# Scan layer of a hybrid decoder trunk: masked products in column pairs with the decay matrix moving, copied out and turned back

## The chip, the cores and the metric

The kernel runs on one core of one Trainium2 chip. The metric is the device time of one launch in microseconds, lower is better. The core's engines are TensorE (PE in the profile, with its weight loads on a row of their own, PEld), VectorE (DVE), ScalarE (ACT), GpSimd (POOL) and SyncE (SP). Each works through its own instructions in the order in which the program lists them; where two engines depend on each other, the later one waits on a semaphore. So an instruction that waits also holds back everything listed behind it on the same engine.

## What is computed

The trunk has two layers of 256 tokens and 1024 features: feed-forward, mixer, feed-forward, each followed by a layer norm. The mixer of the first layer is sparse attention, that of the second a Mamba-2 scan with 32 heads of 64 features in 4 groups of 8 heads, computed in two chunks of 128 tokens. The part that matters here:

```python
    cb = jnp.einsum('bclgn,bcsgn->bcgls', cm, bm)
    y_diag = jnp.einsum('bcgrls,bcsgrp->bclgrp', cb[:, :, :, None] * decay, xdt)
    ...
    y_off = jnp.einsum('bclgn,bcgrpn->bclgrp', cm, prev) * jnp.exp(a_cs_l)[..., None]
    return (y_diag + y_off).reshape(bsz, seq, n_h, p_dim)
...
    y = y + xs.astype(jnp.float32) * d_skip.astype(jnp.float32)[:, None]
    yz = y.reshape(bsz, seq, SSM_INNER) * jax.nn.silu(z.astype(jnp.float32))
    yz = yz.reshape(bsz, seq, SSM_GROUPS, SSM_INNER // SSM_GROUPS)
    yz = yz * lax.rsqrt(jnp.mean(jnp.square(yz), -1, keepdims=True) + RMS_EPS)
```

`y_diag` is, for every head and chunk, a 128x128 matrix (decay times `cb`, masked to the lower triangle) times a 128x64 matrix of inputs. All values are float32.

## The kernel before

Weights come from DRAM as float32 tiles of 128x1024 ("units"). Each unit is split into a high part `wh` (a cast on ACT, line 326, or line 324 where a scale goes in) and a low part `wl` (a subtraction on DVE, line 354 or 351; for a few units ACT negates the raw tile, line 332, and a DMA adds to it). A projection then takes three products instead of one (lines 539, 540 and 541). Ten units may be split ahead of their use. This splitting is most of the work of ACT and DVE, and it is spread over the program by calls of `W.pump`.

The scan layer is the function `ssd`. Its last stage is a loop over the four groups `g`, in an order that is written out by hand. Two threads run through it. One is long projection work for PE, in pieces called fillers, `f[0]` to `f[7]`: for groups 0 and 1 four projections of input tiles for the next group (`xs_tile`, 24 matmuls of 256 columns, ended by a convolution on ACT and DVE in `conv`) and four halves of the gate projection (`z_half`, 12 matmuls of 512 columns); for group 2 a mixture of input tiles and output products (`out_piece`, 12 matmuls of 512 columns); for group 3 output products alone. The other thread is the group's own chain, for the two token tiles t = 0 and 1, placed between the fillers:

- `x_tok` turns the group's inputs to tokens by features and makes `y[t]` (inputs times dt) and `xd[t]` (inputs times the skip factor).
- `decay_load`, `decay_seg`, `decay_exp` and `decay_cb` make the masked decay matrix `M[t, g]`, 128 x (8 heads x 128), by a DMA from POOL's queue, DVE, ACT and DVE.
- `diag` multiplies: for each head the 128x128 slice of `M` is the stationary operand, 64 columns of `y[t]` move, and the result lands with tokens on the partitions.
- `carry` adds what the first chunk hands to the second: one matmul, then two DVE operations on `xe` and `xd[1]`.
- `gate` (DVE) adds `diag`'s result in PSUM to `xd[t]` and multiplies by the gate; `square` (ACT) sums squares; `root` (POOL, two operations) makes the inverse root; `norm` (ACT) scales.
- `y_tr` turns the result back on PE with four transposes and splits it (`yH` on ACT, `yL` on DVE, lines 535 and 536) for the output products.

In PSUM the helper `ptr` hands out two banks in turn, `pmm` two others, and `acc00` to `acc11` are four single ones; at the end the output products accumulate in all four `acc` banks. From group 2 on, `out_piece(0)` therefore needs `acc11`, which `x_tok(0, g)` uses for g < 3.

Of the kernel before, what the change touches and what calls it, by code (L numbers as in the profile page):

```python
# [11 lines left out]
F32 = mybir.dt.float32  # L12
# [400 lines left out]
def trunk_kernel(ctx: ExitStack, tc: tile.TileContext, widths, forms, x, ln_g, ln_b, wts, kvg, convp,  # L413
                 dt_bias, a_log, d_skip, norm_g, out):
    nc = tc.nc
# [5 lines left out]
    psum = ctx.enter_context(tc.tile_pool(name="psum", bufs=1, space=bass.MemoryType.PSUM))  # L421
# [4 lines left out]
    def nm(s):  # L426
        cnt[0] += 1
        return f"{s}_{cnt[0]}"

    def f4(s):  # L430
        return wk.tile([128, 1024], F32, name=nm(s), tag="f4", bufs=12)

    def f2(s):
        return wk.tile([128, 512], F32, name=nm(s), tag="f2", bufs=9)
# [4 lines left out]
    def r2(s):  # L439
        return wk.tile([128, 512], F32R, name=nm(s), tag="r2", bufs=10)  # L440

    def tiny(s, n=32):
        return wk.tile([128, n], F32, name=nm(s), tag=f"tiny{n}", bufs=14 if n == 32 else 4)
# [4 lines left out]
    def pmm():  # L448
        return psum.tile([128, 512], F32, name=nm("pmm"), tag="pmm", bufs=2)
# [11 lines left out]
    def ptr():  # L461
        return psum.tile([128, 512], F32, name=nm("ptr"), tag="ptr", bufs=2)
# [22 lines left out]
    ident = consts.tile([128, 128], F32, name="ident")  # L485
# [35 lines left out]
    def rsqrt_pool(src, eps, scale=1.0):  # L521

        n = src.shape[1]
        e = tiny("rse")
        nc.gpsimd.tensor_scalar(e[:, :n], src, float(scale), float(eps), op0=ALU.mult, op1=ALU.add)
        return power_pool(e[:, :n])
# [7 lines left out]
    def split_psum(H, L, ps):  # L534
        nc.scalar.copy(H, ps)
        nc.vector.tensor_sub(L, ps, H.bitcast(F32))  # L536
# [841 lines left out]
    def ssd(xT, u, ln_i):  # L1378
# [85 lines left out]
        def z_half(g, t, i, uu):  # L1464

            if not i:
                zps[t] = ptr() if t and g == 1 else pmm()
            ps = zps[t]
            for k in range(4 * i, 4 * i + 4):
                H, L = W.get(uu + k // 2)  # L1470
                c = slice((k % 2) * 512, (k % 2 + 1) * 512)
                sl = slice(t * 128, (t + 1) * 128)
                mm3(ps, xT.H[:, k, sl], xT.L[:, k, sl], H[:, c], L[:, c], k == 0, k == DK - 1)
                if t and k % 2:
                    W.free(uu + k // 2)
            if i:
                if not t:
                    zs[g] = f4("zs")
                nc.scalar.activation(zs[g][:, t * 512:(t + 1) * 512], ps, AF.Silu)
# [3 lines left out]
        def decay_load(t, g):  # L1483
            M[t, g] = f4("M")
            nc.gpsimd.dma_start(M[t, g], scr[t:t + 1, g * 8:(g + 1) * 8, :].rearrange("o h l -> o (h l)")
                                .to_broadcast([128, 1024]))
# [49 lines left out]
        def hv(ap):  # L1536
            return ap.rearrange("p (h d) -> p h d", h=8)

        def hb(ap, g):
            return ap[:, g * 8:(g + 1) * 8][:, :, None].to_broadcast([128, 8, 64])  # L1540

        def decay_seg(t, g):

            mv = M[t, g].rearrange("p (h l) -> p h l", h=8)
            nc.vector._custom_dve(TENSOR_ADD_SAT, out=mv, in0=mv, s0=0.0, s1=-3e38,
                                  in1=nacs[t][:, g * 8:(g + 1) * 8][:, :, None].to_broadcast([128, 8, 128]))
# [7 lines left out]
                                 .to_broadcast([128, 8, 128]))  # L1554

        yT = {}
        y, xd, xe, ss = {}, {}, {}, {}

        def x_tok(t, g):

            if t:
                pt = ptr()
            elif g < 3:
                pt = psum.tile([128, 512], F32, name=nm("pxt"), tag="acc11", bufs=1)
            else:
                pt = pmm()
            for i in range(4):
                nc.tensor.transpose(pt[:, i * 128:(i + 1) * 128], xsT[g][i][:, t * 128:(t + 1) * 128], ident)
            y[t], xd[t] = f2("xdt"), f2("xtok")
            nc.vector.tensor_mul(hv(y[t]), hv(pt), hb(dt[:, t * 32:(t + 1) * 32], g))  # L1570
            nc.vector.tensor_mul(hv(xd[t]), hv(pt), hb(dsk, g))
# [3 lines left out]
            nc.vector.tensor_mul(hv(xe[g]), hv(y[0]), hb(dend, g))  # L1575

        def diag(t, g):
            m = M.pop((t, g))
            py = psum.tile([128, 512], F32, name=nm("py"), tag="acc11", bufs=1) if t and g < 2 else ptr()
            for h in range(8):  # L1580
                nc.tensor.matmul(py[:, h * 64:(h + 1) * 64], m[:, h * 128:(h + 1) * 128],
                                 y[t][:, h * 64:(h + 1) * 64], start=True, stop=True)
            return py

        def carry(g):

            po = ptr()
            nc.tensor.matmul(po, cross[:, g * 128:(g + 1) * 128], xe[g], start=True, stop=True)
            nc.vector.tensor_mul(hv(xe[g]), hv(po), hb(eacs, g))
            nc.vector.tensor_add(xd[1], xd[1], xe[g])  # L1590

        def gate(t, g, py):
            nc.vector.tensor_add(y[t], py, xd[t])
            nc.vector.tensor_mul(y[t], y[t], zs[g][:, t * 512:(t + 1) * 512])

        def square(t):
            ss[t] = tiny("ss")
            nc.scalar.activation(xd[t], y[t], AF.Square, accum_out=ss[t][:, 0:1])

        def root(t):  # L1600
            ss[t] = rsqrt_pool(ss[t][:, 0:1], RMS_EPS, 1.0 / 512)

        def norm(t):
            nc.scalar.activation(y[t], y[t], AF.Copy, scale=ss[t])

        def y_tr(t, g):
            pt = ptr()
            for i in range(4):
                nc.tensor.transpose(pt[:, i * 128:(i + 1) * 128], y[t][:, i * 128:(i + 1) * 128], ident)
            yT[g, t] = (r2("yH"), r2("yL"))  # L1610
            split_psum(*yT[g, t], pt)

        def xs_tile(g, i, uu):
            if not i:
                xsT[g] = []
            ps = xbank() if g < 3 else pmm()
            proj_b(ps[:, :256], xT, uu, False)
            W.free(uu)
            o = wk.tile([128, 256], F32, name=nm("xsT"), tag="xsT", bufs=5)
            conv(ps, g * 4 + i, o)  # L1620
            xsT[g].append(o)
            W.pump(1)

        def out_piece(k, uu):
            if not acc:
                acc.update(accs())
            for t in range(2):
                H, L = yT[k // 4, t]
                s = slice(k % 4 * 128, (k % 4 + 1) * 128)
                out_k(acc, t, H[:, s], L[:, s], uu, k == 0, False)  # L1630
            W.free(uu)
            W.pump(1)
# [40 lines left out]
        decay_exp(1, 0)  # L1673
        W.lows()
        u += 4
        py = {}
        for g in range(SG):
            if g < 2:
                f = [lambda i=i: xs_tile(g + 1, i, u + i) for i in range(4)]
                f += [lambda t=t, i=i: (z_half(g + 2, t, i, u + 4), W.pump(1)) for t in range(2) for i in range(2)]  # L1680
            elif g == 2:
                x3 = [lambda i=i: xs_tile(3, i, u + 2 * i) for i in range(4)]
                o0 = [lambda i=i: out_piece(i, u + 2 * i + 1) for i in range(4)]
                f = [x3[0], x3[1], o0[0], x3[2], o0[1], x3[3], o0[2], o0[3]]
            else:
                f = [lambda i=i: out_piece(4 + i, u + i) for i in range(6)]
            f[0]()
            if g:
                x_tok(0, g)
                x_tok(1, g)  # L1690
            else:
                decay_cb(0, 0)
                decay_cb(1, 0)
            x_end(g)
            f[1]()
            f[2]()
            py[0] = diag(0, g)
            gate(0, g, py[0])
            carry(g)
            if g < 3:  # L1700
                decay_load(0, g + 1)
            f[3]()
            square(0)
            root(0)
            py[1] = diag(1, g)
            gate(1, g, py[1])
            if g < 3:
                decay_load(1, g + 1)
            f[4]()
            norm(0)  # L1710
            square(1)
            root(1)
            if g < 3:
                decay_seg(0, g + 1)
            f[5]()
            y_tr(0, g)
            norm(1)
            if g < 3:
                decay_seg(1, g + 1)
                f[6]()  # L1720
                flush()
                y_tr(1, g)
                decay_exp(0, g + 1)
                decay_exp(1, g + 1)
                f[7]()
                decay_cb(0, g + 1)
                decay_cb(1, g + 1)
                W.lows()
                u += 8
# [56 lines left out]
```

## Time and profile before

| | us |
|---|---|
| median of 3 runs (lowest to highest) | 1010.6 (1009.81 to 1010.91) |
| span of the profiled execution | 1009.0 |
| PE busy | 999.1 (99%) |
| PE weight loads busy | 845.8 (84%) |
| DVE busy | 905.3 (90%) |
| ACT busy | 662.0 (66%) |
| POOL busy | 109.8 (11%) |
| group loop of the scan: first `diag` to last `y_tr` | 708.7 to 812.9 in the span |

The span is measured from the first to the last instruction of one profiled execution; the runs are timed without the profiler, and their median lies 1.6 us above that span. No time of its own is listed for the profiled execution. The profile's chain of work says which engine each stretch of the span waited on; its timeline lists instructions with start, duration and, in brackets, how long the engine had been idle and who released it. A matmul's duration in such a row includes its way through the array, so what a stream of matmuls costs is read from the starts of successive rows. One float32 matmul of the program appears as two rows' worth of matmuls in the trace (8 heads are x16).

### The profile page before, as it was taken

To read this page: it belongs to the slowest core of one execution; us is meant where nothing else is said; L and a number is where in the kernel's file an instruction comes from. 1 tells how busy PE (TensorE), PEld (TensorE's weight loads), DVE (VectorE), ACT (ScalarE), POOL (GpSimd) and SP (SyncE) were. 2 spreads that over 40 slices of the span, in tenths; PEclk is the share of its full clock that TensorE was granted. 3 is DMA by queue.
4 is the path that set the end of the run, shared out by engine and by line. 5 is a ranking of instruction groups with operands and counts; after the bars stand their busy time and mean duration, and the time that the engine had idled before them with its cause. 6 is when DMAs were issued, how large, how long until landed. Compare 5 with 4: busy or idle time off the path is not lost.

```text
span 1009.0 us, 14555 instructions
## 1 busy us (share of the span) xinstructions
PE 999.1 (99%) x5273; PEld 845.8 (84%) x5273; DVE 905.3 (90%) x1224; ACT 662.0 (66%) x968; POOL 109.8 (11%) x149
## 2 busy tenths in 40 slices
PE   9999999999999999999999999999999999999997
PEld 6888888898788888888888888999888888888886
DVE  7899999888898999999899998788989978899996
ACT  6676776476755767764576776486876645676670
POOL 0010110100000101100010110150221100010100
PEclk9999999999999999999999999999999999999999
DMA  9799889551754998995499889457765754699981
GB/s 347 224 289 284 240 254 334 195 172 57 245 173 126 274 280 241 260 390 183 123 281 288 243 253 357 168 179 241 222 215 181 235 191 136 170 265 285 289 254 42
DMA packets 66055, 231.69 MB, mean 230 GB/s; under 512 B 8112, under 2 KB 9136, under 8 KB 65984
## 3 DMA queue, kind: packets, MB, share of 16 engines
q1 hardware_dynamic: 54288, 189.84, 51.7%
q0 software_dynamic: 11120, 40.41, 21.7%
q8 instruction: 41, 0.67, 0.3%
q10 hardware_dynamic: 576, 0.52, 0.2%
q14 instruction: 30, 0.25, 0.1%
HBM read 193.48 MB, written 1.08 MB: 193 GB/s over the span
## 4 chain that ended last, share of the span: by engine, by line
PE 94%; DVE 3%; DMA 1%; issue 1%; POOL 0%; ACT 0%; DVEq 0%; POOLq 0%; SPq 0%
PE pmm L539 12%; PE pmm L540 12%; PE pmm L541 12%; PE acc L539 10%; PE acc L541 10%; PE acc L540 10%; PE ptr L539 2%; PE ptr L541 2%; PE ptr L540 2%; PE pxs L539 2%; PE pxs L541 2%; PE pxs L540 2%; PE pmm L705 1%; PE ptr L705 1%; PE ptr L795 1%; PE pmm L685 1%
## 5 line engine op out<-in xcount | busy, mean ns | idle before, releaser
L354 DVE TENSOR_TENSOR wl<-raw,wh 128x1024 fp32r<-128x1024 f32 (+3 forms) x424 | 495.5, 1211 | 14.6 <-ACT wh L326 14.1
L326 ACT CAST wh<-raw 128x1024 fp32r<-128x1024 f32 (+2 forms) x431 | 428.8, 1043 | 91.8 <-DVE raw L293 51.1
L539 PE MATMUL acc<-wh,hH 128*128 128x512 f32 (+1 forms) x352 | 138.1, 392 | 0.0
L541 PE MATMUL acc<-wh,hL 128*128 128x512 f32 (+1 forms) x352 | 136.5, 388 | 0.0
L540 PE MATMUL acc<-wl,hH 128*128 128x512 f32 (+1 forms) x352 | 136.3, 387 | 0.0
L539 PE MATMUL pmm<-wh,xT 128*128 128x512 f32 (+2 forms) x304 | 119.2, 392 | 0.0
L541 PE MATMUL pmm<-wh,xT 128*128 128x512 f32 (+2 forms) x304 | 116.9, 384 | 0.0
L540 PE MATMUL pmm<-wl,xT 128*128 128x512 f32 (+2 forms) x304 | 116.7, 384 | 0.1
L266 POOL DMA_DIRECT2D raw<-raw x64 | 55.8, 877 | 490.3 <-DVE raw L293 260.4
L541 PE MATMUL pmm<-wh,xf 128*128 128x512 f32 x256 | 99.6, 389 | 0.0
L539 PE MATMUL pmm<-wh,xf 128*128 128x512 f32 x256 | 99.6, 389 | 0.0
L540 PE MATMUL pmm<-wl,xf 128*128 128x512 f32 x256 | 99.6, 389 | 0.0
L541 PEld LDWEIGHTS acc<-wh,hL 128*128 128x128 f32 x352 | 66.1, 188 | 13.7
L293 DVE TENSOR_TENSOR raw<-raw,raw 128x1024 f32<-128x1024 f32 x64 | 77.0, 1218 | 0.2
L540 PEld LDWEIGHTS acc<-wl,hH 128*128 128x128 f32 x352 | 66.2, 188 | 12.9
L539 PEld LDWEIGHTS acc<-wh,hH 128*128 128x128 f32 x352 | 66.1, 188 | 12.8
L541 PEld LDWEIGHTS pmm<-wh,xT 128*128 128x128 f32 x304 | 57.0, 188 | 11.9 <-DVE xT L536 0.5
L540 PEld LDWEIGHTS pmm<-wl,xT 128*128 128x128 f32 x304 | 57.2, 188 | 11.0 <-DVE wl L354 0.8
L539 PEld LDWEIGHTS pmm<-wh,xT 128*128 128x128 f32 x304 | 57.1, 188 | 10.0
L541 PEld LDWEIGHTS pmm<-wh,xf 128*128 128x128 f32 x256 | 48.0, 188 | 10.0
L539 PEld LDWEIGHTS pmm<-wh,xf 128*128 128x128 f32 x256 | 48.0, 188 | 10.0
L540 PEld LDWEIGHTS pmm<-wl,xf 128*128 128x128 f32 x256 | 48.0, 188 | 10.0
(321 smaller groups left out, 1784.6 us busy)
## 6 DMA issues: line engine op xcount, KB each, us to landing
raw<-in_wts_dram SPq DMA_DIRECT2D x338, 512.0 KB, 5.9
raw<-raw POOLq DMA_DIRECT2D x64, 512.0 KB, 5.4
M<-scr POOLq DMA_DIRECT2D x8, 512.0 KB, 6.0
lng<-in_ln_g_dram SPq DMA_DIRECT2D x6, 512.0 KB, 5.5
lnb<-in_ln_b_dram SPq DMA_DIRECT2D x6, 512.0 KB, 5.9
wl<-raw POOLq DMA_DIRECT2D x5, 512.0 KB, 5.5
raw<-in_wts_dram SPq DMA_DIRECT2D x4, 408.0 KB, 5.4
out_dram<-x SPq DMA_DIRECT2D x4, 256.0 KB, 2.0
```

The lines of the kernel that those rows point to most:

```text
L266: self.nc.gpsimd.dma_start(self.raw[r], self.raw[other], accum_op=ALU.add)
L293: self.nc.vector.tensor_add(self.raw[r], self.raw[r], self.raw[other])
L326: nc.scalar.copy(h[:, c:c + n], raw[:, c:c + n])
L354: self.nc.vector.tensor_sub(lo[:, s], raw[:, s], h[:, s].bitcast(F32))
L539: nc.tensor.matmul(ps, lh, rh, start=first, stop=False, skip_group_check=on)
L540: nc.tensor.matmul(ps, lh, rl, start=False, stop=False, skip_group_check=on)
L541: nc.tensor.matmul(ps, ll, rh, start=False, stop=last, skip_group_check=on)
L685: nc.tensor.matmul(ps, a, b[:, c], start=k == i == 0, stop=k == DK - 1 and i == 2)
L705: nc.tensor.matmul(ps, H[:, k * 128:(k + 1) * 128], xT.HL[:, k, :], start=k == 0, stop=False)
L795: nc.tensor.transpose(v[:, i, t * 128:(t + 1) * 128], hs[t][:, i * 128:(i + 1) * 128], ident)
```

## The change

`diag` swaps its operands. Now 64 columns of `y[t]` are stationary and the 128x128 slice of `M` moves; even heads write partitions 0 to 63 and odd heads 64 to 127 of the same PSUM columns. The result therefore lands with features on the partitions. ACT copies it from PSUM to a new tile `ydT` (`turned[t]`), and a new function `back` turns it with four transposes into another PSUM bank, from which `gate` reads. `diag(0)` and `diag(1)` now stand together before `carry`; both `decay_load`s follow them at once; `back(0)`, `back(1)` and both gates, squares and roots stand behind `f[3]`; both `norm`s behind `f[4]`; and for g < 3 `y_tr(0)` and `y_tr(1)` both stand behind `f[5]`. Of the PSUM banks, `x_tok(0, 2)` moves from `acc11` to `ptr`, and `diag(1, g)` takes `pmm` for g of 2 and 3.

```diff
-        y, xd, xe, ss = {}, {}, {}, {}
+        y, xd, xe, ss, turned = {}, {}, {}, {}, {}
...
             if t:
                 pt = ptr()
-            elif g < 3:
+            elif g < 2:
                 pt = psum.tile([128, 512], F32, name=nm("pxt"), tag="acc11", bufs=1)
             else:
-                pt = pmm()
+                pt = ptr() if g < 3 else pmm()
...
         def diag(t, g):
+
             m = M.pop((t, g))
-            py = psum.tile([128, 512], F32, name=nm("py"), tag="acc11", bufs=1) if t and g < 2 else ptr()
-            for h in range(8):
-                nc.tensor.matmul(py[:, h * 64:(h + 1) * 64], m[:, h * 128:(h + 1) * 128],
-                                 y[t][:, h * 64:(h + 1) * 64], start=True, stop=True)
+            if not t:
+                py = ptr()
+            else:
+                py = psum.tile([128, 512], F32, name=nm("py"), tag="acc11", bufs=1) if g < 2 else pmm()
+            for j in range(4):
+                for h in (2 * j, 2 * j + 1):
+                    p0 = (h % 2) * 64
+                    nc.tensor.matmul(py[p0:p0 + 64, j * 128:(j + 1) * 128], y[t][:, h * 64:(h + 1) * 64],
+                                     m[:, h * 128:(h + 1) * 128], start=True, stop=True)
+            turned[t] = f2("ydT")
+            nc.scalar.copy(turned[t], py)
+
+        def back(t):
+            a, py = turned.pop(t), ptr()
+            for j in range(4):
+                nc.tensor.transpose(py[:, j * 128:(j + 1) * 128], a[:, j * 128:(j + 1) * 128], ident)
             return py
...
             f[2]()
-            py[0] = diag(0, g)
-            gate(0, g, py[0])
-            carry(g)
+            diag(0, g)
+            diag(1, g)
             if g < 3:
                 decay_load(0, g + 1)
+                decay_load(1, g + 1)
+            carry(g)
             f[3]()
-            square(0)
-            root(0)
-            py[1] = diag(1, g)
-            gate(1, g, py[1])
-            if g < 3:
-                decay_load(1, g + 1)
+            py = [back(0), back(1)]
+            for t in range(2):
+                gate(t, g, py[t])
+                square(t)
+                root(t)
             f[4]()
             norm(0)
-            square(1)
-            root(1)
+            norm(1)
             if g < 3:
                 decay_seg(0, g + 1)
             f[5]()
             y_tr(0, g)
-            norm(1)
             if g < 3:
+                y_tr(1, g)
                 decay_seg(1, g + 1)
                 f[6]()
                 flush()
-                y_tr(1, g)
                 decay_exp(0, g + 1)
                 decay_exp(1, g + 1)
                 f[7]()
```

How the instructions then stand is shown for group 1 on the two engines between `f[3]` and `y_tr`. First ACT before, from the convolution's first step of `f[3]` (line 1498) to the cast of `y_tr(0, 1)`: line 1598 is `square`, line 1604 `norm`, `xdt` is `y[t]`, `zs` the gate of a filler.

```order
L1498 ACTIVATE cv_7486<-pxs_7460,convp_sb 128x256
L1493 ACTIVATE xsT_7430<-cv_7431 128x256
L324 ACTIVATE wh_7495<-raw_7310,ng_sb 128x1024
L1598 ACTIVATE xtok_7354,ss_7498<-xdt_7353 128x512
L326 CAST wh_7533<-raw_7400 128x1024
L1604 ACTIVATE xdt_7353<-xdt_7353,rs_7502 128x512
L1598 ACTIVATE xtok_7363,ss_7537<-xdt_7362 128x512
L1479 ACTIVATE zs_7556<-pmm_7517 128x512
L324 ACTIVATE wh_7561<-raw_7438,ng_sb 128x1024
L535 CAST yH_7569<-ptr_7564 128x512
```

The same stretch of ACT in the changed kernel, where line 1590 is the copy of `diag`'s result, 1611 `square` and 1617 `norm`:

```order
L1590 COPY ydT_7466<-ptr_7457 128x512
L1590 COPY ydT_7477<-py_7468 128x512
L1498 ACTIVATE cv_7513<-pxs_7487,convp_sb 128x256
L1493 ACTIVATE xsT_7444<-cv_7445 128x256
L324 ACTIVATE wh_7522<-raw_7324,ng_sb 128x1024
L1611 ACTIVATE xtok_7368,ss_7537<-xdt_7367 128x512
L1611 ACTIVATE xtok_7377,ss_7545<-xdt_7376 128x512
L326 CAST wh_7567<-raw_7414 128x1024
L1617 ACTIVATE xdt_7367<-xdt_7367,rs_7541 128x512
L1617 ACTIVATE xdt_7376<-xdt_7376,rs_7549 128x512
L1479 ACTIVATE zs_7585<-pmm_7551 128x512
L324 ACTIVATE wh_7590<-raw_7452,ng_sb 128x1024
```

The cast of `y_tr(0, 1)` follows. The two copies are new, and `norm` of tile 0, which stood behind the first square alone, now stands behind both squares. DVE before, from the last weight of `f[2]` to the second gate (lines 1593 and 1594 are `gate`, 1589 and 1590 `carry`, 1501 the three further steps of a convolution):

```order
L351 SCALAR_TENSOR_TENSOR wl_7403<-raw_7271,ng_sb,wh_7402 128x1024
L1593 TENSOR_TENSOR xdt_7353<-ptr_7443,xtok_7354 128x512
L1594 TENSOR_TENSOR xdt_7353<-xdt_7353,zs_6344 128x512
L1589 TENSOR_TENSOR xe_7366<-ptr_7454,eacs_6238 128x512
L1590 TENSOR_TENSOR xtok_7363<-xtok_7363,xe_7366 128x512
L1501 SCALAR_TENSOR_TENSOR cv_7486<-pxs_7460,convp_sb,cv_7486 128x255
L1501 SCALAR_TENSOR_TENSOR cv_7486<-pxs_7460,convp_sb,cv_7486 128x254
L1501 SCALAR_TENSOR_TENSOR cv_7486<-pxs_7460,convp_sb,cv_7486 128x253
L354 TENSOR_TENSOR wl_7441<-raw_7302,wh_7440 128x1024
L1593 TENSOR_TENSOR xdt_7362<-py_7504,xtok_7363 128x512
L1594 TENSOR_TENSOR xdt_7362<-xdt_7362,zs_6344 128x512
```

DVE in the changed kernel, where lines 1602 and 1603 are `carry`, 1606 and 1607 `gate`:

```order
L351 SCALAR_TENSOR_TENSOR wl_7417<-raw_7294,ng_sb,wh_7416 128x1024
L1602 TENSOR_TENSOR xe_7380<-ptr_7483,eacs_6238 128x512
L1603 TENSOR_TENSOR xtok_7377<-xtok_7377,xe_7380 128x512
L1501 SCALAR_TENSOR_TENSOR cv_7513<-pxs_7487,convp_sb,cv_7513 128x255
L1501 SCALAR_TENSOR_TENSOR cv_7513<-pxs_7487,convp_sb,cv_7513 128x254
L1501 SCALAR_TENSOR_TENSOR cv_7513<-pxs_7487,convp_sb,cv_7513 128x253
L354 TENSOR_TENSOR wl_7455<-raw_7316,wh_7454 128x1024
L1606 TENSOR_TENSOR xdt_7367<-ptr_7525,xtok_7368 128x512
L1607 TENSOR_TENSOR xdt_7367<-xdt_7367,zs_6344 128x512
L1606 TENSOR_TENSOR xdt_7376<-ptr_7530,xtok_7377 128x512
L1607 TENSOR_TENSOR xdt_7376<-xdt_7376,zs_6344 128x512
```

The first gate has moved from ahead of the carry to behind the convolution and the weight of `f[3]`; the number of DVE operations is the same.

More of the change, by code (lines that the diff above doesn't have):

```diff
@@ L1675, in ssd @@
         u += 4
-        py = {}
         for g in range(SG):
```

## The prediction

> **What bounds the kernel now.** First the page's span, busy time by engine and chain of work, then the list of what PE waited for, then one window over the scan's group loop.
>
> ```profile
> span 1009.0 us, 14555 instructions
> PE 999.1 (99%) x5273; PEld 845.8 (84%) x5273; DVE 905.3 (90%) x1224; ACT 662.0 (66%) x968; POOL 109.8 (11%) x149
> PE 94%; DVE 3%; DMA 1%; issue 1%; POOL 0%; ACT 0%; DVEq 0%; POOLq 0%; SPq 0%
> PE acc L539 <- DVE xtok L1571: 0.9, 1, 0.9
> 700.00:820.00 120.00, 119.06 (x745) 105.23 (x744) 105.91 (x141) 80.09 (x111) 19.11 (x26) 1.00 0.68 217
> ```
>
> The chain is PE for 94%, and in the whole group loop PE waits once that this view counts, 0.9 us on `x_tok`. So PE's own list is the clock here: a microsecond off its work is a microsecond gained, and each wait put into it is lost whole. DVE is busy 105.91 of 120 us, so it has little room to catch up.
>
> **The products.** Group 1's rows on PE, then the one place that already multiplies in this form, the attention's `po` (64 stationary columns, heads on partitions 0 and 64 in turn), and the eight transposes of one `x_tok`.
>
> ```profile
> 737.48 1.90 PE L1581 MATMUL ptr<-xdt,M 128*128 128x64 f32 x16
> 739.22 1.08 PE L1588 MATMUL ptr<-xe,cross 128*128 128x512 f32 x2
> 743.00 1.90 PE L1581 MATMUL py<-xdt,M 128*128 128x64 f32 x16
> 744.70 0.47 PE L539 MATMUL pmm<-wh,xT 128*128 128x512 f32 x1
> 271.31 0.40 PE L541 MATMUL acc<-wh,oL 128*128 128x512 f32 x1
> 271.64 1.97 PE L1248 MATMUL po<-pT,v 128*64 128x128 f32 x32
> 273.54 0.50 PE L539 MATMUL acc<-wh,oH 128*128 128x512 f32 x1
> 273.88 0.39 PE L540 MATMUL acc<-wl,oH 128*128 128x512 f32 x1
> 759.54 0.60 PE L1568 MATMUL pxt<-ident,xsT 128*128 128x128 f32 x4
> 759.98 0.60 PE L1568 MATMUL ptr<-ident,xsT 128*128 128x128 f32 x4
> 760.33 0.36 PE L539 MATMUL pmm<-xT,wh 128*128 128x256 f32 x1
> ```
>
> From start to start the two `diag`s of a group take 739.22 - 737.48 = 1.74 and 744.70 - 743.00 = 1.70 us. In the new form 32 such matmuls took 273.54 - 271.64 = 1.90 us, and the switch of form cost about 0.1 going in (0.33 from 271.31 instead of the 0.23 of a 512-column product in its stream, rows below) and 0.1 coming out (0.34 from 273.54). Both `diag`s together are these 32: 2.1 instead of 3.5 us with the 0.09 that the step after `diag(1)` loses now. That is -1.4 us a group, **-5.6 us** in four. The bounds are 0 (no pairing, each matmul at the old 0.11) and -5.6; I take the row, since shapes and order of partitions are the same.
>
> The turns add eight transposes a group: 760.33 - 759.54 = 0.79 us, with 0.09 for the switch 0.88; **+3.5 us** in four. The Trainium skill, "TensorE: Matmul & The Clock Gate", section "Part 4: PE-mode transpose", gives about 275 ns for one 128x128 transpose inside a kernel; by that figure the 32 turns would be 8.8 us and the total 5.3 us higher. The rows show four in 0.60 us with the way through the array, and eight in 0.79 from start to start; the measurement decides.
>
> Two smaller terms. `out_piece(0)` no longer needs the bank of `x_tok(0, 2)`; the rows here are the matmul before that wait and three after:
>
> ```profile
> 765.12 0.39 PE L541 MATMUL acc<-wh,yL 128*128 128x512 f32 x1
> 766.38 0.47 PE L539 MATMUL acc<-wh,yH 128*128 128x512 f32 x1 [0.87 <-DVE xtok L1571]
> 766.69 0.40 PE L540 MATMUL acc<-wl,yH 128*128 128x512 f32 x1
> 766.92 0.39 PE L541 MATMUL acc<-wh,yL 128*128 128x512 f32 x1
> ```
>
> 1.26 from start to start instead of the 0.23 of the last two: **-1.0 us**. Behind it `diag(0, 2)` could be late instead, on the same `x_tok`; the lead that DVE gets from the stalls below pays for that. And `diag(1, 0)` now asks for its `M` 1 us after `diag(0, 0)`, while DVE makes the two in turn, each as large as a weight (1.22 us below): **+0.2 us**. The two `y_tr` side by side save a switch of form, 3 x 0.09: **-0.3 us**. Sum on PE's list: -5.6 + 3.5 - 1.0 + 0.2 - 0.3 = **-3.2 us**.
>
> **The new wait.** Before, `y_tr(0)` came two products and a carry behind its gate, and `y_tr(1)` stood behind one filler more. Now both come behind only `back`, `f[4]` and `f[5]`, while gate, square, root and norm of both tiles must fit into that. Rows of group 1 on PE, ACT, DVE and POOL (the last two for groups 2 and 1) give the length of that chain, counted from the end of `f[3]` on PE (743.00, where `diag(1)` begins):
>
> ```profile
> 750.28 0.60 PE L1609 MATMUL ptr<-ident,xdt 128*128 128x128 f32 x4
> 753.49 0.60 PE L1609 MATMUL ptr<-ident,xdt 128*128 128x128 f32 x4
> 743.20 0.56 ACT L1498 ACTIVATE cv<-pxs,convp_sb 128x256 f32<-128x256 f32 x1 [2.30 <-PE pxs L541]
> 745.62 1.03 ACT L326 CAST wh<-raw 128x1024 fp32r<-128x1024 f32 x1
> 747.73 0.72 ACT L1604 ACTIVATE xdt<-xdt,rs 128x512 f32<-128x512 f32 x1 [1.08 <-POOL rs L531]
> 748.63 0.63 ACT L1598 ACTIVATE xtok<-xdt 128x512 f32<-128x512 f32 x1 [0.18 <-DVE xdt L1594]
> 749.17 0.19 ACT L1598 ACTIVATION_READ_ACCUMULATOR xtok<-xdt 128x1 f32 x1
> 744.63 1.51 DVE L1501 SCALAR_TENSOR_TENSOR cv<-pxs,convp_sb,cv 128x255 f32<-128x255 f32 x3
> 746.06 1.22 DVE L354 TENSOR_TENSOR wl<-raw,wh 128x1024 fp32r<-128x1024 f32 x1
> 747.19 0.68 DVE L1593 TENSOR_TENSOR xdt<-py,xtok 128x512 f32<-128x512 f32 x1
> 748.52 1.28 DVE L351 SCALAR_TENSOR_TENSOR wl<-raw,ng_sb,wh 128x1024 fp32r<-128x1024 f32 x1
> 745.81 0.19 POOL L525 TENSOR_SCALAR rse<-ss 128x1 f32<-128x1 f32 x1 [9.32 <-ACT xtok L1598]
> 746.08 1.62 POOL L531 TENSOR_TENSOR rs<-rse,mhalf 128x1 f32<-128x1 f32 x1
> 775.75 0.56 POOL L531 TENSOR_TENSOR rs<-rse,mhalf 128x1 f32<-128x1 f32 x1
> 743.97 1.14 ACT L324 ACTIVATE wh<-raw,ng_sb 128x1024 fp32r<-128x1024 f32 x1
> ```
>
> ACT's first convolution step ends 0.76 behind 743.00. In the new order DVE then does the other three (746.06 - 744.63 = 1.43), a weight (747.19 - 746.06 = 1.13) and two gates (748.52 - 747.19 = 1.33 each): 6.0. The second square takes until 749.36, 0.76 behind its gate: 6.7. Behind it on ACT stands a weight cast of 1.03: 7.8; then `norm(0)`, 0.72: **8.5 us**. The root of tile 0 is ready by then: its square ends at 5.4, and from square to norm POOL took 2.0 (745.7 to 747.73). PE comes to `y_tr(0)` after `back` (0.8) and the two fillers (750.28 - 744.70 = 5.6): 6.4. So PE **stands 2.1 us** there. `norm(1)` needs the second root, 6.7 + 2.0 = 8.7 if POOL takes it at once, 9.3 if it stands behind the first root, then 0.72 more, while PE is ready for `y_tr(1)` at 8.9: 0.6 to 1.2 us more. POOL has also done the root's second step in 0.56 instead of 1.62 us, so I keep 0.3 as the low end. A group's stall is 2.1 + 0.8 = **2.9**, from 2.4 to 3.3.
>
> Group 2 has an input tile as `f[3]` and `f[5]` and scaled weights (1.14 on ACT); chain and filler both grow by 0.15, so 2.9 again. In group 0 two things are longer:
>
> ```profile
> 717.79 1.05 ACT L332 ACTIVATE wl<-raw 128x1024 fp32r<-128x1024 f32 x1
> 720.16 0.69 DVE L1594 TENSOR_TENSOR xdt<-xdt,zs 128x512 f32<-128x512 f32 x1
> 721.59 0.60 PE L1609 MATMUL ptr<-ident,xdt 128*128 128x128 f32 x4
> ```
>
> DVE is behind there: its work up to the second gate is the same as before in another order, and that ended at 720.85. Square (0.76), cast (1.03), the negated weight (1.05, also between square and norm) and norm (0.72) lead to 724.4. PE, which came to `y_tr(0)` at 721.59, would come 0.5 earlier (-1.4 + 0.2 + 0.8). So 3.3, and 0.3 for the second tile: **3.6 us** (3.2 to 4.0). Group 3 has no convolution; without 0.76 + 1.43 + 1.13, but with the 0.4 of `back(0)` ahead of the gate, its chain is 2.9 us shorter: no stall. In all 2 x 2.9 + 3.6 = **+9.4 us**, from 8.0 to 10.6.
>
> **What costs nothing.** ACT's eight copies are of 0.6 us each and fall into idle time such as the 2.30 us in front of the 743.20 row; `back` comes a filler later and finds them done. `decay_load(1)` can be issued when its product ends, at 739.6 by the rows above instead of 744.7, so POOL's queue has it out long before the roots behind it, and DVE gets `M` sooner. ACT and DVE stand while PE does, so weights are split later, but ten units may be ahead. In group 2 the cast of `y_tr(1)` must wait until `out_piece(3)` has read the buffer that it takes over, now one filler (753.49 - 750.28, less the turn, 2.8 us) longer than before. Behind that cast on ACT stand the exponentials that lead to `M` of group 3, and on DVE its inputs. `diag(0, 3)` comes four fillers later, some 11 us, which I take as cover enough; without it up to the 2.8 us would go to PE.
>
> **The sum.** 1009.0 - 3.2 + 9.4 = 1015.2 us of span. The runs' median stands 1.6 above the span, so **1016.8 us**. The bounds of the stalls give 1015.4 to 1018.0, the cover in group 2 nearly 1021.
>
> **Rivals.**
> - *The norms are in time.* If the chain were 2.1 us shorter per group, PE would not stand at all and only the list counts: 1010.6 - 3.2 = 1007.4, faster. It decides where `norm(0)` ends 6.4 us behind `f[3]`; the rows say 8.5, each link being one that this trace shows. For it speaks only that DVE idles at times, so its backlog is not always there. Chance 0.06.
> - *Half of the stalls.* If squares and casts overlap better or POOL's roots are all quick, or if PE's lost time lets something later go faster, 1010 to 1013. Against it: PE waits nowhere else for more than the 0.9 us, so there is nothing to win back. Chance 0.07, most of it within 0.2%.
> - *The clock.* At the start of the trace, after PE's first wait, come slow matmuls:
>
> ```profile
> 1.24 2.32 PE L492 MATMUL ptr<-blank 128*128 128x512 bf16 x5 [1.24 <-DVE half L483]
> 0.00:4.00 4.00, 2.75 (x7) 1.05 (x8) 0.28 (x2) 1.31 (x2) 2.07 (x13) 1.00 0.46 145
> ```
>
>   Five of 512 columns from 1.24 to the next row's start at 3.57 are 0.47 each against 0.23 later, though the window's row gives the granted clock as 1.00. If a stall of 3 us brought PE back to that rate for some 3 us, each would cost 1.5 us more: three stalls, 1021. The Trainium skill, "TensorE: Matmul & The Clock Gate", section "Part 1: The HAM clock gate", says that an idle window of about 3.4 us halves the clock; our stalls are split by `y_tr(0)` and mostly below that, and no stall that long is in the trace. Chance 0.08.
> - *No pairing.* The swapped products stay at 0.11 each: +5.6, 1022. The `po` rows speak against it. Chance 0.03.
>
> My forecast has 0.76. The range leaves out the first two rivals and the last (0.16) and reaches to the clock's: 1013.0 to 1021.5. Differences of 0.2% (2 us) are about what a measurement of this kernel can tell from none. Faster: 0.06; within: 0.05; slower: 0.89.
>
> **What would show it.** In the changed trace: the x32 row of the products taking about 1.9 us; PE's list of waits headed by `ptr` at line 1622 (`y_tr`), released by ACT's `xdt` of line 1617, some 3 us in each of groups 0 to 2 and nothing in group 3; no wait on `x_tok` any more; the idle time of ACT ahead of line 1611 ended by DVE. I would be wrong if `norm` ended before PE got to line 1622, or if PE waited at the products or for weights instead.

## The result and the profile after

The changed kernel takes **1023.2 us** (median of 4 runs, 1021.0 to 1023.9) against 1010.7 us before: 1.0122 times as long, 95% interval 1.0108 to 1.0136. It is slower, as forecast, but by 12.5 us and not by 6.1. From the page of the changed kernel, the three lines that answer to those of before:

```profile
span 1022.2 us, 14633 instructions
PE 1002.2 (98%) x5305; PEld 845.3 (83%) x5305; DVE 905.8 (89%) x1224; ACT 666.6 (65%) x976; POOL 111.1 (11%) x149
PE 88%; DVE 7%; DMA 2%; ACT 1%; issue 1%; POOL 1%; SPq 0%; DVEq 0%; POOLq 0%
```

PE is busy for 3.1 us longer, though its list was to become 3.2 us shorter, and the chain now runs through DVE for 7% instead of 3%. The waits of PE (engine and line that waited, who ended it, us in all, times, the longest):

```profile
PE ptr L1622 <- ACT xdt L1617: 8.9, 5, 2.9
...
PE acc L539 <- ACT yH L535: 0.7, 1, 0.7
PE pmm L685 <- ACT wh L326: 0.7, 1, 0.7
PE pxT L557 <- DMA x<-in_x_dram: 0.6, 1, 0.6
```

The first is the forecast's wait at `y_tr`, 8.9 us where the forecast had 9.4; the second is a small one in group 3 that the forecast didn't name, and with it the sum is 9.6. `x_tok` is gone from the list. The last two lie ahead of the scan, in the first 100 us. The rest shows in stretches of the group loop (the last three figures of a row: granted clock of PE, DMA share, GB/s):

```profile
720.00:730.00 10.00, 7.07 (x28) 5.43 (x27) 6.43 (x9) 7.85 (x13) 4.12 (x5) 0.83 0.78 223
760.00:770.00 10.00, 10.00 (x51) 8.60 (x51) 7.15 (x8) 9.38 (x12) 0.00 (x0) 0.83 0.42 150
790.00:800.00 10.00, 8.90 (x37) 7.20 (x38) 5.48 (x8) 5.91 (x11) 1.16 (x2) 0.83 0.42 136
```

Before, the granted clock over the loop was 1.00. Now it is 0.83 in the stretches behind the three stalls, and in 760 to 770 PE is busy all the time and yet does only 51 instructions. The rows of group 0 behind the first stall (start, length, engine and line, operation, count):

```profile
725.08 1.42 PE L1622 MATMUL ptr<-ident,xdt 128*128 128x128 f32 x8 [2.93 <-ACT xdt L1617]
726.15 0.78 PE L539 MATMUL pmm<-wh,xT 128*128 128x512 f32 x1
726.72 0.63 PE L540 MATMUL pmm<-wl,xT 128*128 128x512 f32 x1
727.15 0.63 PE L541 MATMUL pmm<-wh,xT 128*128 128x512 f32 x1
...
729.61 0.39 PE L541 MATMUL pmm<-wh,xT 128*128 128x512 f32 x1
729.84 0.39 PE L539 MATMUL pmm<-wh,xT 128*128 128x512 f32 x1
```

Read the starts, since the lengths contain the way through the array: 726.72 and 727.15 are 0.43 us apart, the last two rows 0.23. A product of 512 columns goes at about half the rate for 3.5 us behind the stall. Over nominal spacing this costs 1.6 us in group 0, 1.6 in group 1 and 1.2 in group 2 (its transposes included).

The starts of the masked products lay the whole difference out by groups (PE's rows of lines 1581 and 1587; "rest" runs from those of group 3 to the end; the other columns are runs told below):

| from start to start, us | before | changed | fed | gates first | norms first |
|---|---|---|---|---|---|
| group 0 to 1 | 28.75 | 33.18 | 31.57 | 30.73 | 28.39 |
| group 1 to 2 | 29.67 | 33.51 | 31.92 | 29.31 | 29.85 |
| group 2 to 3 | 28.49 | 31.91 | 30.85 | 29.12 | 27.72 |
| rest | 213.4 | 214.0 | 213.9 | 213.9 | 214.2 |

The changed kernel loses 4.4, 3.8, 3.4 and 0.6 us, and 0.9 ahead of the loop, where the two waits near the start of this execution lie, which that of before hadn't: 13.1, the two spans' difference of 13.2 but for rounding.

### The profile page after: what moved, and what is told of

Its sections match the earlier page's. It is cut to its first block, busy times and chain, and to the rows that moved or that the text cites. A ratio compares the mean times of both kernels' runs of the same rounds, so it can differ in the third digit from the quotient of the medians.

```text
span 1022.2 us, 14633 instructions
## 1 busy us (share of the span) xinstructions
PE 1002.2 (98%) x5305; PEld 845.3 (83%) x5305; DVE 905.8 (89%) x1224; ACT 666.6 (65%) x976; POOL 111.1 (11%) x149
## 4 chain that ended last, share of the span: by engine, by line
PE 88%; DVE 7%; DMA 2%; ACT 1%; issue 1%; POOL 1%; SPq 0%; DVEq 0%; POOLq 0%
PE pmm L539 12%; PE pmm L540 12%; PE pmm L541 12%; PE acc L539 9%; PE acc L541 9%; PE acc L540 9%; PE ptr L539 2%; PE ptr L541 2%; PE ptr L540 2%; PE pxs L539 2%; PE pxs L541 2%; PE pxs L540 2%; PE pmm L705 1%; DVE wl L354 1%; PE ptr L705 1%; PE ptr L795 1%
## 5 line engine op out<-in xcount | busy, mean ns | idle before, releaser
L539 PE MATMUL pmm<-wh,xT 128*128 128x512 f32 (+2 forms) x304 | 120.4, 396 | 0.0
L541 PE MATMUL pmm<-wh,xT 128*128 128x512 f32 (+2 forms) x304 | 118.1, 388 | 0.0
```

Source lines behind the costliest of these rows:

```text
L539: nc.tensor.matmul(ps, lh, rh, start=first, stop=False, skip_group_check=on)
L541: nc.tensor.matmul(ps, ll, rh, start=False, stop=last, skip_group_check=on)
```

## The experiments

All are compared with the kernel before, run beside them on the same chip (its median was 1010.2 to 1010.7 in every set). Differences from the changed kernel's 1023.2 us are differences of medians from two sets; by the ratios to before they come out up to 0.6 us smaller, and the interval of each ratio reaches 0.9 to 1.4 us to either side.

### Feeding PE through the stall

```diff
 def y_tr(t, g):
     pt = ptr()
+    for i in range(((14, 0), (10, 7), (9, 3), (0, 0))[g][t]):
+        nc.tensor.matmul(pt[:, :128], ident, ident, start=True, stop=True)
```

> The changed kernel with unused 128x128 products of the identity put into the bank of y_tr right ahead of its transposes: 14 and 0 in group 0, 10 and 7 in group 1, 9 and 3 in group 2, about 0.22 us each, so that PE works through most of the time in which it stood. Their results are overwritten. Theory (the idle time itself halves the clock): the norms come as late as before, but the products behind y_tr take 0.23 instead of 0.43 us; 4 to 5 us less than the changed kernel, about 1018.5. Rival (the half clock has another cause): 1023 or, with what of the unused products hangs over, up to 1026.

1019.1 us, ratio 1.0086 (1.0073 to 1.0099): 4.1 us less than the changed kernel, by doing 43 unused products more. Its stretches and its rows of the same place:

```profile
720.00:730.00 10.00, 10.00 (x63) 8.80 (x62) 6.46 (x8) 9.37 (x15) 4.12 (x5) 1.00 0.65 187
760.00:770.00 10.00, 10.00 (x72) 9.40 (x71) 8.93 (x11) 8.64 (x11) 0.61 (x1) 1.00 0.39 120
```

```profile
723.97 1.22 PE L1624 MATMUL ptr<-ident,xdt 128*128 128x128 f32 x8
724.94 0.48 PE L539 MATMUL pmm<-wh,xT 128*128 128x512 f32 x1
725.26 0.40 PE L540 MATMUL pmm<-wl,xT 128*128 128x512 f32 x1
725.49 0.39 PE L541 MATMUL pmm<-wh,xT 128*128 128x512 f32 x1
```

The clock is 1.00, the products are 0.23 apart at once, and 72 instead of 51 instructions start in 760 to 770 (not quite the same part of the list). The turn still comes 3.4 us behind the last product that counts. So idle time itself brings the half rate, and that part of the loss is some 4 us: 3.6 by the ratios, and 1.6, 1.6 and 1.1 that the groups give back in the table.

### Feeding it through half of the stall

The same with 7, 5 and 5 unused products ahead of `y_tr(0)` and none ahead of `y_tr(1)`.

> The changed kernel with 7, 5 and 5 unused products of the identity ahead of y_tr(0) in groups 0 to 2, none ahead of y_tr(1): PE's first idle time falls to 1.5, 1.1 and 1.0 us, the second stays (0.2, 1.8, 0.8). Theory A (the half clock needs idle time close together of some 2.5 to 3 us): at full clock in groups 0 and 2 and perhaps in group 1, 1018.5 to 1020. Theory B (any idle time of 1 us or more brings it): half clock as before, 1023.

1021.0 us, ratio 1.0101 (1.0087 to 1.0115), 2.2 us less than the changed kernel, though the two intervals overlap; theory A had given 1 us less, 1018.5 to 1020. The trace decides between the theories. Idle spells of 1.56 us in group 0 and of 1.07 and 0.91 in group 2 are followed by full rate; only in group 1, where 1.11 and 1.81 lie on both sides of the four transposes of one turn, come five slow products (0.9 us). Spells of over 1 us alone don't bring the half rate, so theory B falls. Theory A holds: the two spells of group 1 are 2.9 us close together, those of groups 0 and 2 at most 2.0.

### The order without the new products, and the reverse

Old products, no copy and no turn, in the new order:

```diff
-    for j in range(4):
-        for h in (2 * j, 2 * j + 1):
...
-    turned[t] = f2("ydT")
-    nc.scalar.copy(turned[t], py)
+    for h in range(8):
+        nc.tensor.matmul(py[:, h * 64:(h + 1) * 64], m[:, h * 128:(h + 1) * 128],
+                         y[t][:, h * 64:(h + 1) * 64], start=True, stop=True)
+    return py
```

> The new order with the old products: each masked product again with M as stationary operand, no copy and no turn, gates read the products' bank. Theory (the order makes the stalls; the turns only delay PE's arrival by 0.8 us a group): products +5.6, turns -3.5, stalls at y_tr longer by 0.8 in groups 0 to 2 (+2.4), clock as in the changed kernel: about 1027 to 1028, waits at line y_tr of 3 us or more in each of groups 0 to 2. Rival (the gates are late because they wait for copy and turn): no stalls, about 1012 to 1013.

1030.5 us, ratio 1.0198 (1.0185 to 1.0211). The order alone does the damage, 20 us against before; the 2 to 3 us beyond the expectation are longer waits (11.8 instead of 8.9, where 2.4 more were expected) and more of the half clock (0.81, 0.85, 0.83, 0.89 and 0.94 in the stretches behind the waits):

```profile
PE ptr L1619 <- ACT xdt L1614: 11.8, 5, 3.8
```

The reverse, new products with copies and turns in the old order, with each `back` at the nearest place that the old order has:

```diff
     diag(0, g)
+    carry(g)
+    gate(0, g, back(0))
     f[3]()
     square(0); root(0)
     diag(1, g)
     f[4]()
+    gate(1, g, back(1))
```

> The new products, copies and turns in the old order: diag(0), carry, back(0), gate(0), f[3], square, root, diag(1), f[4], back(1), gate(1); y_tr(0) behind f[5] and y_tr(1) behind f[6] as in the kernel before. Theory (products and turns cost what their rows say; only the order makes stalls): -5.6 for the products, +1.2 for switching form twice as often, +3.5 turns, -1.0 for the wait on x_tok: about 1009, and no half clock. Rival (the products or turns themselves bring the half clock or late gates): 1013 or more, with windows at 0.83.

1019.5 us, ratio 1.0087 (1.0073 to 1.0101): the expectation of 1009 is missed, by a fault of the edit:

```profile
PE ptr L1595 <- ACT ydT L1590: 4.3, 2, 2.2
PE ptr L1601 <- DVE xe L1575: 1.7, 3, 0.6
```

`back(0)` 1.1 us behind its product waits for the copy, which stands on ACT behind work that waits for DVE:

```profile
745.19 0.42 ACT L1493 ACTIVATE xsT<-cv 128x256 f32<-128x256 f32 x1 [2.30 <-DVE cv L1501]
745.52 1.03 ACT L326 CAST wh<-raw 128x1024 fp32r<-128x1024 f32 x1
746.45 0.58 ACT L1590 COPY ydT<-ptr 128x512 f32<-128x512 f32 x1
```

The rival's signs, over 1013 us and a stretch at 0.83 (710 to 720), are there too, but the waits come from the copy's place on ACT in this order. So a copy of 0.6 us needs a filler between product and turn, as the change gives it; the run doesn't price the products alone. That is done further down.

### What makes the norms late

The forecast's chain went through convolution and weight work of `f[3]` ahead of the gates. Here `back`, gates, squares and roots are put between its products and its convolution:

```diff
-def xs_tile(g, i, uu):
+def xs_tile(g, i, uu, between=None):
...
     W.free(uu)
+    if between:
+        between()
...
     conv(ps, g * 4 + i, o)
```

> The changed kernel with back, gates, squares and roots of groups 0 to 2 put between f[3]'s products and its convolution, which now stands behind them with its weights. Theory (convolution and weight ahead of the gates, 0.76 + 1.43 + 1.13 us, make the norms late): the waits at y_tr fall to under 1 us a group, no window of 0.83, 1008 to 1011. Rival (DVE's and ACT's whole load sets it, whatever the order; the convolution is then late for the next step): 1015 to 1023, with waits for cv or xsT.

1015.6 us, ratio 1.0047 (1.0035 to 1.0060), 7.6 us less than the changed kernel, and no clock below 1.00 behind a stall. The time lies in the rival's range, without the rival's waits for `cv` or `xsT`; of the theory the full clock came, but the waits at `y_tr` stay, 2.1 us in group 0 and 1.0 in the next two:

```profile
PE ptr L1622 <- ACT xdt L1617: 4.1, 3, 2.1
```

ACT's rows in group 1, up to the two norms:

```profile
750.67 1.14 ACT L324 ACTIVATE wh<-raw,ng_sb 128x1024 fp32r<-128x1024 f32 x1
751.72 1.03 ACT L326 CAST wh<-raw 128x1024 fp32r<-128x1024 f32 x1
752.65 1.33 ACT L1617 ACTIVATE xdt<-xdt,rs 128x512 f32<-128x512 f32 x2
```

No idle time is shown: the norms stand behind two weights on a busy ACT. The next run takes the roots out of the changed kernel, which tells POOL's part:

```diff
 def root(t):
-    ss[t] = rsqrt_pool(ss[t][:, 0:1], RMS_EPS, 1.0 / 512)
+    ss[t] = ss[t][:, 0:1]
```

> The changed kernel without the two POOL steps of the root: norm scales by the sum of squares itself, so the output differs and two small POOL instructions per tile are left out. Theory (y_tr(0) waits for the row of convolution, weight, gates, square and cast on DVE and ACT; only y_tr(1) waits for the roots, which POOL does one after the other): the first tile's waits stay at 3.1, 2.2 and 2.1 us, the second's (0.2, 1.9, 0.8) go, and in groups 1 and 2 part of the half clock with them: 1018 to 1020. Rival (POOL's root sets both): nearly all waits go, about 1009 to 1012. Rival (POOL sets nothing): 1023.

1017.1 us, ratio 1.0069 (1.0055 to 1.0083), 0.9 below the range expected:

```profile
PE ptr L1622 <- ACT xdt L1617: 6.9, 3, 2.9
```

Three waits instead of five: the first tile's 3.1, 2.1 and 2.1 us between starts stay as they were, the second's go, and so does the wait for `yH`, which came of a root of group 3 and which the expectation had left out. The clock is now 0.83 in group 0 alone. So the first tile waits for ACT and DVE, and the second for POOL.

### Mending the order

Both turns one filler later, then each one later than in the changed kernel by one and two fillers:

```diff
 f[5]()
-y_tr(0, g); y_tr(1, g)
 decay_seg(1, g + 1)
 f[6]()
 flush()
+y_tr(0, g); y_tr(1, g)
```

In the second of the two runs `y_tr(0, g)` stands there, and `y_tr(1, g)` behind `f[7]`.

> Both y_tr of groups 0 to 2 stand one filler later (behind f[6]); products, copies and turns as changed. Theory (the two y_tr come about 2 to 3 us ahead of the norms; each stall costs its length, 10 us over groups 0 to 2, and half the PE clock for some 3 us behind it, 4.9 us in all): waits at line 1622 below 1 us in each group, no 10 us window at 0.83, about 1008 us. Rival (the half clock comes from the 64-column products and the turns, not from the stalls): the waits go, the 0.83 windows stay, about 1013. Rival (the cost lies in more work on ACT and DVE, which shows wherever PE asks next): 1018 to 1023.

1015.7 us, ratio 1.0060 (1.0047 to 1.0072). The half clock is gone, as the theory has it and against the first rival; the 1008 us are missed, since waits remain under other names, as the second rival has it:

```profile
PE ptr L1622 <- ACT xdt L1617: 2.1, 3, 1.2
PE pmm L539 <- ACT zs L1479: 1.8, 1, 1.8
PE acc L539 <- ACT yH L535: 1.0, 1, 1.0
```

> y_tr(0) behind f[6], y_tr(1) behind f[7] in groups 0 to 2, the exponentials between them. Theory (in the run with both behind f[6] the rest was 0.9 and 1.4 us for the second norm, 2.0 us for a Silu behind the exponentials and 1.2 us for yH): the second norm's waits go, the Silu's too since the turn's casts no longer stand ahead of the exponentials; about 1010 to 1011. Rival (ACT, with the copies on top, is late in any order): the waits only take other names, about 1015.

1025.2 us, ratio 1.0151 (1.0137 to 1.0165), worse than the changed kernel itself, which neither theory nor rival had. The waits are longer, and the half clock is back (0.83 in 740 to 750, 0.69 in 770 to 780). Behind `f[7]` the turn's casts stand on ACT and DVE ahead of what the next group's `x_tok` and products ask for:

```profile
PE ptr L1568 <- DVE yL L536: 5.3, 1, 5.3
PE ptr L1587 <- DVE xdt L1570: 5.1, 2, 4.0
```

So moving the turn back isn't the remedy; bringing the norms forward is. On top of the run with the gates first, both norms stand right behind the convolution, ahead of the weights, and no longer behind `f[4]`:

```diff
     conv(ps, g * 4 + i, o)
     xsT[g].append(o)
+    if between:
+        norm(0)
+        norm(1)
     W.pump(1)
```

> The run with the gates first, and both norms of groups 0 to 2 right behind the convolution of f[3], ahead of the weight work of f[3] and f[4], behind which they stood by 1.2 to 2.2 us too long. Theory (with the norms in time only PE's list is left, 3.2 us shorter than before): waits at y_tr below 0.3 us a group, 0.8 for yH in group 3 stays, no half clock; 1007.5 to 1009, 1.5 to 3 us below before. Rival (weights, convolution or M are then late, DVE and ACT being short of time): waits at the next products, 1010 to 1014.

**1010.9 us**, ratio 1.0006 (0.9997 to 1.0015). The forecast of 1007.5 to 1009 is missed, and the rival's 1010 to 1014 holds. No wait at `y_tr` is left:

```profile
PE pmm L539 <- ACT zs L1479: 0.8, 1, 0.8
PE acc L539 <- ACT yH L535: 0.7, 1, 0.7
PE ptr L1595 <- DVE xe L1602: 0.2, 1, 0.2
```

12.3 us of the loss (11.7 by the ratios) are undone by order alone, with every product, copy and turn in place; the 3.2 us that PE's list is shorter are eaten by waits that weren't there before: from start to start 1.0 for `zs`, 0.8 for `yH`, 0.5 at `back` of group 1, and 0.3 twice between the products of `diag`, 2.9 in all. The same kernel with the old products:

> The same order with the old products (M stationary), no copy, no turn; the gates read the products' banks and stand between f[3]'s products and its convolution. Theory (pairs save 5.6 us on PE, turns cost 3.5): 2 us more than the run with the new products, about 1009.5 to 1011. Rival (copies and turns cost more than their rows, through ACT or the way through two more banks): the same or less than the run with the new products.

1012.5 us, ratio 1.0017 (1.0008 to 1.0026). The new products are worth 1.6 us here; the intervals against before overlap a little, but each of these 11 runs (1011.93 and more) is slower than each of the other kernel's 11 (1011.91 and less), and the spans differ by 1.9 (1010.9 and 1009.0). Forecast were 2.1 (5.6 less 3.5), from which the waits at `diag` and `back` come off.

Two more waits were then taken away: the second norm of group 3 behind `y_tr(0, 3)` again, and the exponentials of group 1 behind `f[7]`, so that a Silu isn't behind them.

> The run with the norms first, with two more steps moved: the second norm of group 3 behind y_tr(0, 3), as in the kernel before, and the exponentials of group 1 behind f[7], so that the Silu that frees a bank doesn't stand behind them and their table load. Theory (what hid the 3.2 us in that run were these two waits, 0.8 to 1.0 us each): both go, 1.5 to 2 us less, about 1009 us, 0.1 to 0.2% below the kernel before. Rival (M of group 2 is then late at its products): 1010.5 to 1012.

1010.4 us, ratio 0.9997 (0.9988 to 1.0006): not to be told from before. Both waits are gone and another stands there:

```profile
PE ptr L1587 <- DVE xtok L1571: 1.0, 1, 1.0
```

DVE, which first stood 1.25 us for the exponentials now moved, worked without a break from 760.92 to the end of that `xtok` at 767.1, and PE came at 766.2. So the time is about the rival's, but not by its cause: `M` was ready at 763.3. The product waited for its bank, one of `ptr`'s, which `x_tok(0, 2)` uses since the change and which this `xtok` reads last. The bank of `x_tok(0, 2)` alone, put into the kernel before:

```diff
-    elif g < 3:
+    elif g < 2:
         pt = psum.tile([128, 512], F32, name=nm("pxt"), tag="acc11", bufs=1)
     else:
-        pt = pmm()
+        pt = ptr() if g < 3 else pmm()
```

> The kernel before with one line of the change, the bank of x_tok(0, 2) taken from ptr instead of the output's fourth accumulator. Theory (the wait of 0.9 us was for that bank): no wait on x_tok, 1.0 us less than before, about 1009.6. Rival (diag(0, 2) or the turns then wait for a ptr bank): no gain, 1010.5 to 1012.

1010.4 us, ratio 0.9998 (0.9989 to 1.0007). The wait is gone from the list and the profiled span is 1007.8 instead of 1009.0, but the medians show 0.1 us. A gain of 1 us lies just within the interval, so it stays open. No version was shown faster than the kernel before.

## Why the prediction was wrong

**The products** were right. In group 1:

```profile
742.82 1.09 PE L1587 MATMUL ptr<-M,xdt 128*64 128x128 f32 x16
743.75 1.04 PE L1587 MATMUL py<-M,xdt 128*64 128x128 f32 x16
744.72 1.13 PE L1601 MATMUL ptr<-xe,cross 128*128 128x512 f32 x2
748.55 1.03 PE L1595 MATMUL ptr<-ident,ydT 128*128 128x128 f32 x8
749.34 0.47 PE L539 MATMUL pmm<-wh,xT 128*128 128x512 f32 x1
```

The 32 take 744.72 - 742.82 = 1.90 us, as in the attention, so that rival (no pairing) falls. In group 0 they took 0.26 longer, the 0.2 for `M`. **The turns** are 0.79 us a group, 749.34 - 748.55; the 275 ns each of the Trainium skill ("TensorE: Matmul & The Clock Gate", "Part 4: PE-mode transpose") would have been 2.2 as an estimate, so the trace doesn't agree.

**The stalls** at `y_tr` were right in mechanism, and in sum 8.9 against 9.4, though the sum is partly luck: the groups miss in both directions. The chain of group 1 on DVE, ACT and POOL, with PE's two arrivals:

```profile
749.35 1.52 DVE L1501 SCALAR_TENSOR_TENSOR cv<-pxs,convp_sb,cv 128x255 f32<-128x255 f32 x3 [1.67 <-ACT cv L1498]
750.78 1.22 DVE L354 TENSOR_TENSOR wl<-raw,wh 128x1024 fp32r<-128x1024 f32 x1
754.69 0.63 ACT L1611 ACTIVATE xtok<-xdt 128x512 f32<-128x512 f32 x1 [0.60 <-DVE xdt L1607]
755.32 1.03 ACT L326 CAST wh<-raw 128x1024 fp32r<-128x1024 f32 x1
756.30 0.72 ACT L1617 ACTIVATE xdt<-xdt,rs 128x512 f32<-128x512 f32 x1
754.79 1.48 POOL L531 TENSOR_TENSOR rs<-rse,mhalf 128x1 f32<-128x1 f32 x1
757.12 1.41 POOL L531 TENSOR_TENSOR rs<-rse,mhalf 128x1 f32<-128x1 f32 x1
758.56 0.72 ACT L1617 ACTIVATE xdt<-xdt,rs 128x512 f32<-128x512 f32 x1 [1.53 <-POOL rs L531]
757.08 0.66 PE L1622 MATMUL ptr<-ident,xdt 128*128 128x128 f32 x4 [2.02 <-ACT xdt L1617]
759.33 0.66 PE L1622 MATMUL ptr<-ident,xdt 128*128 128x128 f32 x4 [1.60 <-ACT xdt L1617]
```

From `back`'s start at 748.55 the first norm ends after 757.02 - 748.55 = 8.5 us, as forecast. The second is ready at 759.28, 10.7 instead of 9.4 to 10.0: POOL takes the roots one after the other, 1.4 to 1.5 us for the second step of each. So group 1 was under-sized (3.6 against 2.9), groups 0 and 2 over-sized (2.9 against 3.6; 2.4 against 2.9), and group 3's stall of 0.7, a norm waiting for its root ahead of the cast of `yH`, was missed. The run with the gates first shows the chain's first links to be a cause, the run with the norms first its last ones, and the run without roots that the second tile waits for POOL. From start to start the stalls cost 0.1 to 0.2 us more each than the waits' list says: the list counts from the end of the last product's row, 0.39 us behind its start, where the next product would have started after 0.23.

**The clock is the step that failed.** The forecast left it out of the sum and gave it 0.08 as a rival, with the ground that "our stalls are split by `y_tr(0)` and mostly below that, and no stall that long is in the trace". Its price was good: 1.5 us for each of three stalls, against 1.6, 1.6 and 1.2 measured, and some 4 by the run that fed PE. The total of that rival, 1021, is within 2.2 us of the measured 1023.2; the forecast's 1016.8 with 3.6 to 4.4 added gives 1020.4 to 1021.2, and the 0.9 ahead of the loop belongs to no part of the change.

The ground failed because neither the split nor the length decides. Read in steps of 0.01 us, the granted clock of the changed kernel falls to 0.50 at 726.07, 760.20 and 790.92 and is back at 1.00 after 3.41 us each time. The three falls are 34.13 and 30.72 us apart, 10 and 9 times 3.413. In every other trace with more than one fall, counting the one behind its last product, they lie whole multiples of that apart too. So in these traces the clock is set anew on a fixed grid of 3.41 us, which doesn't start with the stall. Three steps of that grid around group 1's stall (PE's busy time is the second figure behind the range, the clock the third from the end):

```profile
753.38:756.79 3.41, 1.68 (x8) 1.06 (x6) 3.38 (x4) 2.81 (x6) 2.45 (x3) 1.00 0.61 216
756.79:760.20 3.41, 1.52 (x10) 1.25 (x11) 1.33 (x2) 1.88 (x4) 1.65 (x2) 1.00 0.94 253
760.20:763.61 3.41, 3.41 (x10) 2.64 (x9) 2.30 (x3) 2.88 (x5) 0.00 (x0) 0.50 0.32 129
```

PE stood 1.73 us in the first step, and the clock stayed; it stood 1.89 in the second, and the third ran at half. Ahead of the falls in groups 0 and 2 it stood 2.42 and 1.97 us of a step. In group 2 the clock fell 0.23 us into the first turn, before the second wait began, so there one spell of 2.0 us was enough. Laid over all 14 traces from 12 to 990 us, every step at full clock with 1.89 us or more of idle time is followed by half rate, and none with 1.73 or less is. What counts here, with transposes taken as work, is thus idle time of over about half of one step, in one piece or two: a stall of 2.0 us in one step brings it, and one of 2.1 us across two steps, as in group 0 of the run with the gates first, doesn't. The forecast had no means to place its stalls on the grid, so that all three were hit is in part chance. The Trainium skill, "TensorE: Matmul & The Clock Gate", section "Part 1: The HAM clock gate", has an idle window of about 3.4 us that runs freely. The traces agree in the window's length and that it runs freely, but not that it must be idle throughout; the measurement decides.

**The rest.** The wait for `x_tok` is gone, though its value isn't shown by the run with that edit alone. The cover in group 2 held: there is no stall for the yielded buffers. "Norms in time" would have given 1007.4; the run that has them in time gives 1010.9, mostly because of the 2.9 us of waits named above, by which that rival's sum was too good.

## What to carry to other kernels

Before work that PE waits for is moved, count its chain link by link on the in-order engines, with what merely stands ahead there: the same two norms cost 12 us or nothing, depending on whether a convolution and weight casts stood ahead of their steps. A stall of PE of 2 us or more, also one in two pieces, can have a second price of 1.2 to 1.6 us, in half-rate products behind it, and belongs in the sum. A shorter list on PE is worth only what the next waits leave of it: here the waits took 2.9 of 3.2 us, and the time shows no gain at all (1.0006).

## What the runs showed of the hardware

- Unused products can pay: 43 fp32 products of 128x128 in time that was lost anyway made the kernel about 4 us faster than without them, by keeping the clock at 1.00.
- In these traces PE's clock was halved in steps of 3.41 us on a grid fixed for the execution, each time behind a step in which PE had stood for 1.89 us or more, and never behind one at full clock with 1.73 or less.
- POOL's second step of a root, on 128x1, took 1.41 to 1.48 us in six of its eight places in the changed kernel's loop and 0.55 in two; in the run with the gates first it took 0.55 to 0.57 in groups 0 to 2 and 1.41 to 1.47 in group 3. It is the same instruction each time; the cause stays open.
